# Inverse square roots as one GpSimd power operation, and the low halves of ten weight blocks made in the feed-forward before the mixers

## The chip, the cores and the metric

One core of a Trainium2 chip runs the whole program in one launch. The metric is the device time of one execution in microseconds (us); less is better. The kernel before takes 1023.36 us (median of 3 runs, 1023.26 to 1024.52).

## What is computed

Two layers act on x of 256 tokens by 1024 columns, in float32. Each layer is a feed-forward with half weight, three token mixers side by side, and a second feed-forward:

```
x = x + 0.5 * swiglu(rms_norm(x, norm_ffn1), ffn1_w13, ffn1_w2)     # 1024 -> 2 x 2816 -> 1024
h = rms_norm(x, norm_mix)
z, xbc, dt_raw, cq, ckv, kidx, widx, xl, gl = split(h @ w_in)       # 1024 -> 2508 columns
y = concat(ssd(z, xbc, dt_raw), attention(cq, ckv, kidx, widx), rg_lru(xl, gl))
x = x + y @ w_out
x = x + 0.5 * swiglu(rms_norm(x, norm_ffn2), ffn2_w13, ffn2_w2)
```

`rms_norm` multiplies by `rsqrt(mean(x*x) + 1e-6)`. It is used for the three norms of the layer, for cq, ckv and kidx (one number per token each), for the heads of q and k (8 per token), and for the two groups of the state-space mixer's output. The attention selects 64 keys per query by an indexer's score. The state-space mixer (SSD) convolves xbc, takes silu of it, and combines it with decays that come from a cumulated sum of softplus(dt_raw); the recurrence (rg_lru) is a scan over time.

## The kernel before

A float32 product is made from three fast products. Each weight tile is split (`wsplit`, L255) into a high half `whi`, a rounded copy by ScalarE (L260), and a low half `wlo`, the rest, by VectorE (L261); `mm3` and `mmt` (L250, L264) then add high times high, high times low and low times high in PSUM. `whi` and `wlo` have four buffers each, the landing place `wraw` of a weight load four as well (1 MB each); the SP queue issues the loads in program order, each as soon as its buffer is free.

A feed-forward (`ffn`, L316) goes over 11 pieces c of 256 columns, with two loads of 1 MB per piece, and then over the second weight in 12 loads. The mixers (`mixers`, L384) project the small columns first (dt, cq, ckv, kidx, widx; L417 to L429), and then, by `pair` (L407), eight pairs of blocks of 128 columns: xl, four pairs of xbc (columns 512, 768, 0 and 256 of it), gl, and two of z. Each block takes 24 products of 256 columns. A pair's sums stand in one of three PSUM buffers named gu until VectorE has multiplied them by the row norms (`scaled`, L685; L727; L773).

Beside these blocks run the small chains of the mixers. For the attention: the squares of cq, ckv and kidx (L438), their inverse roots `sc` (L454), the indexer's queries and keys (L473, L485, L493 to L496), their transposes (L506), scores (L523, L530), eight rounds of taking the eight largest (`select`, L534: MAX and MATCH_REPLACE on VectorE), then the mask, softmax and the weighted values (L592 to L625). For the SSD: a softplus on GpSimd in some thirty small steps (L634 to L639), the cumulated sum `pac` on TensorE (L641), the decays M0 and M1 (L647 to L666), the convolutions (L669), of which those of columns 512 and 768 are issued after the selection (`picked`), and the products with the decays. At the end come the out-projections (`project`, L804, matmuls on L807) and the next feed-forward.

An inverse root (`rsqrt`, L158, and `rsqrt_of`, L164) is a first guess from the bits of the number and two steps of Newton's kind, eleven instructions on VectorE counting the first scaling; for the heads of q and k it is on GpSimd, where two of the steps need an extra instruction each time.

The order on each engine is set when the program is built: a scheduler goes through the program text and a model of the engines' times and places each instruction; on the chip each engine then keeps that order strictly and waits where an operand is not there.

Of the kernel before, what the change touches and what calls it, by code (L numbers as in the profile page):

```python
# [7 lines left out]
F32 = mybir.dt.float32  # L8
# [7 lines left out]
P = 128  # L16
# [15 lines left out]
MAGIC = 1597463007.0  # L32
RS = (64.0 / 9.0) ** 2
# [31 lines left out]
def tile_decoder_trunk(ctx: ExitStack, tc: tile.TileContext, A: dict, out: bass.AP):  # L65
# [79 lines left out]


# [11 lines left out]
    def rsqrt(dst, src, scale, pool, tg, E=V):  # L158
# [5 lines left out]
    def rsqrt_of(dst, v, pool, tg, E=V):  # L164


        n = list(dst.shape)
        yi = pool.tile(n, I32, name=tg + "y")
        E.tensor_scalar(yi, v.bitcast(I32), -0.5, MAGIC, ALU.mult, ALU.add)
        v2 = pool.tile(n, F32, name=tg + "h")  # L170
        E.tensor_scalar(v2, v, 9.0 / 64.0, None, ALU.mult)
        y = yi.bitcast(F32)
        for i in range(2):
            t = pool.tile(n, F32, name=tg + "t")
            E.tensor_mul(t, y, y)
            E.tensor_mul(t, t, v if i == 0 else v2)
            stt(E, t, t, -10.0 / 3.0, t, ALU.add, ALU.mult)
            z = dst if i == 1 else pool.tile(n, F32, name=tg + "z")
            last = stt(E, z, t, 5.0, y, ALU.add, ALU.mult)
            y = z  # L180
        return last.ins
# [134 lines left out]
    def ffn(n, w13, w2, pool, finish, first=False):  # L316
# [5 lines left out]
        for c in range(KF // 2):  # L322
# [61 lines left out]
    def mixers(n, l, mp, finish):  # L384
# [5 lines left out]
        ya_, yl_ = two("ya_", 1), two("yl_", 1)  # L390

# [3 lines left out]
        def mix_ps():  # L395
            return psa.tile([P, 512], F32, name="acc")
# [10 lines left out]
        def pair(raw, c0, eng):  # L407
# [43 lines left out]
        for i, dim in enumerate((256, 128, 64)):  # L451
            V.tensor_scalar(vc[:, i], lss[:, i], RS / dim, EPS * RS, ALU.mult, ALU.add)
        sc = mp.tile([P, 3, NH], F32, name="sc", bufs=1)
        rsqrt_of(sc, vc, mp, "cr")  # L454
# [106 lines left out]
        rsqrt(qr, qss, 1.0 / 64, mp, "qq", G)  # L561
# [85 lines left out]
        M0, M1 = [], []  # L647
        for g in range(2):
            m0 = mp.tile([P, 4, SEQ], F32, name="m0", bufs=2)
            m1 = mp.tile([P, 4, P], F32, name="m1", bufs=2)  # L650
            for q in range(2):
                pb = mix_ps()
                for i in range(2):
                    hd = 4 * g + 2 * q + i
                    for h in range(NH):
                        bcast_rows(pb[:, i * SEQ + h * P:i * SEQ + (h + 1) * P], ac[:, h, hd:hd + 1])
                for i in range(2):
                    hd = 4 * g + 2 * q + i
                    S.activation(m0[:, 2 * q + i], pb[:, i * SEQ:(i + 1) * SEQ], AF.Relu, scale=-1.0,
                                 bias=ac[:, 0, hd:hd + 1])  # L660
                    S.activation(m1[:, 2 * q + i], pb[:, i * SEQ + P:(i + 1) * SEQ], AF.Relu, scale=-1.0,
                                 bias=ac[:, 1, hd:hd + 1])
            S.activation(m0, m0, AF.Exp, scale=-1.0)
            S.activation(m1, m1, AF.Exp, scale=-1.0)
            M0.append(m0)
            M1.append(m1)  # L666

# [22 lines left out]
        def xbc_pair(raw, b0, eng, after=None):  # L690
            xr = scaled(pair(raw, 0, eng))
            t = two("xbc", 4)
# [6 lines left out]
        def lru():  # L699
            ps = pair(load_cols(C_XL, 256), 0, (V, V))  # L700
            xr = two("lx", 1)
            conv(xr, scaled(ps), "lru_conv_w", 2, "lru_conv_b", 0)
            la, la2, lt, lb = two("la", 1), two("la2", 1), two("lt", 1), two("lb", 1)
# [20 lines left out]
        def lru_gate(hs):  # L724
            ps = pair(load_cols(C_GL, 256), 0, (V, V))
            gx, hx, gt = two("lx", 1), two("lb", 1), two("lt", 1)
# [8 lines left out]

        hs = lru()


        xbc_pair(load_cols(C_XBC + 512, 256), 4, (V, V), picked)
        xbc_pair(load_cols(C_XBC + 768, 256), 6, (V, V), picked)  # L740

        for g in range(2):
# [4 lines left out]
            cb = mp.tile([P, 3 * P], F32, name="cb", bufs=2)  # L747
# [4 lines left out]
        xbc_pair(load_cols(C_XBC, 256), 0, (V, V))  # L752
        xbc_pair(load_cols(C_XBC + 256, 256), 2, (V, V))

        xdt = []
        for h in range(NH):
# [3 lines left out]
            t = mp.tile([P, 8, 64], F32, name="xdt", bufs=2)  # L760
# [8 lines left out]
        zs, yg = [], []  # L769
        for q in range(2):  # L770
            ps = pair(load_cols(C_Z + 256 * q, 256), 0, (V, V))
            z = two("z", 2)
            V.tensor_mul(z, ps, rb2)  # L773
            silu2(z, z)
            zs.append(z)
# [163 lines left out]
```

## Time and profile before

| | |
|---|---|
| median of 3 runs | 1023.36 us |
| the profiled execution | 1025.87 us |
| its span in the trace | 1024.1 us |
| TensorE (PE) busy | 991.1 us, 97% |
| VectorE (DVE) busy | 661.3 us, 65% |
| ScalarE (ACT) busy | 515.2 us, 50% |
| GpSimd (POOL) busy | 52.7 us, 5% |

The profiled execution took 1025.87 us, of which 1024.1 us are its span, from the first instruction to the last, and 1.8 us lie around it. Matmuls are pipelined: their lengths overlap, so that the distance from one start to the next is what one costs. All times inside are counted from the start of the span. Layer 0's mixers lie at about 206 to 330 us, layer 1's at about 711 to 834 us.

### The profile page before, as it was taken

The numbers are of one execution on the slowest core, as the hardware profiler recorded it, in microseconds if no ns is written. First come the engines' busy times: TensorE is split into PE (matmuls) and PEld (weight loads), VectorE is DVE, ScalarE is ACT, GpSimd is POOL, SyncE is SP. The second block draws the span as 40 slices with busy tenths as digits, with TensorE's granted clock in tenths as the row PEclk, the third lists the DMA queues.
The fourth block names the chain that finished last, engine by engine and source line by source line (L and its number), as shares of the span: only waits on it lengthen the run. The fifth ranks groups of instructions, "written<-read, shape, count | busy, mean of one in ns | idle before, by whom it ended". The sixth has DMA issues, their size and how long they took to land.

```text
span 1024.1 us, 12885 instructions
## 1 busy us (share of the span) xinstructions
PE 991.1 (97%) x4819; PEld 806.0 (79%) x4819; DVE 661.3 (65%) x1158; ACT 515.2 (50%) x806; POOL 52.7 (5%) x133
## 2 busy tenths in 40 slices
PE   7999999999869999999999999999998999999998
PEld 5888888889844888888888888888897468888886
DVE  6666755576977666664576656555889766566543
ACT  6554545468533554544455445455695255454442
POOL 0600000042000000000000000000500000000000
PEclk9999999999989999999999999999998899999999
DMA  9765555743205565555556555557431256564560
GB/s 318 204 201 175 175 186 167 242 148 109 98 27 184 167 197 177 173 195 194 186 159 207 190 175 176 183 197 229 131 125 42 60 187 206 168 201 149 183 224 21
DMA packets 142752, 172.47 MB, mean 168 GB/s; under 512 B 4851, under 2 KB 114577, under 8 KB 142689
## 3 DMA queue, kind: packets, MB, share of 16 engines
q1 hardware_dynamic: 141792, 171.03, 51.9%
q0 software_dynamic: 864, 0.60, 0.4%
q8 instruction: 38, 0.62, 0.2%
q14 instruction: 26, 0.21, 0.1%
q10 hardware_dynamic: 32, 0.01, 0.0%
HBM read 170.57 MB, written 1.05 MB: 168 GB/s over the span
## 4 chain that ended last, share of the span: by engine, by line
PE 83%; DVE 9%; ACT 3%; DMA 2%; POOL 2%; issue 1%; SPq 0%; ACTq 0%; DVEq 0%; POOLq 0%
PE gu L266 16%; PE gu L268 16%; PE gu L267 16%; PE acc L267 8%; PE acc L268 8%; PE acc L266 8%; PE gu L807 3%; DVE wlo L261 2%; DMA wraw<-in_ffn_w_dram 2%; PE sm L356 2%; DVE xbc L674 1%; PE gu L251 1%; DVE score L542 1%; PE gu L253 1%; PE gu L252 1%; PE sm L289 1%
## 5 line engine op out<-in xcount | busy, mean ns | idle before, releaser
L261 DVE TENSOR_TENSOR wlo<-wraw,whi 128x1024 fp32r<-128x1024 f32 (+1 forms) x304 | 370.5, 1221 | 259.0 <-ACT whi L260 252.7
L260 ACT ACTIVATE whi<-wraw 128x1024 fp32r<-128x1024 f32 (+1 forms) x304 | 321.9, 1061 | 283.5 <-PE gu L268 159.3
L266 PE MATMUL gu<-whi,xh 128*128 128x512 f32 (+1 forms) x736 | 289.8, 396 | 2.5 <-ACT whi L260 2.5
L268 PE MATMUL gu<-whi,xl 128*128 128x512 f32 (+1 forms) x736 | 289.0, 396 | 0.0
L267 PE MATMUL gu<-wlo,xh 128*128 128x512 f32 (+1 forms) x736 | 286.6, 391 | 0.0
L267 PEld LDWEIGHTS gu<-wlo,xh 128*128 128x128 f32 x736 | 138.7, 189 | 28.2 <-DVE wlo L261 0.8
L266 PEld LDWEIGHTS gu<-whi,xh 128*128 128x128 f32 x736 | 138.6, 189 | 28.2 <-ACT whi L260 2.9
L268 PEld LDWEIGHTS gu<-whi,xl 128*128 128x128 f32 x736 | 138.5, 188 | 27.6
L268 PE MATMUL acc<-whi,hl 128*128 128x512 f32 x352 | 137.8, 392 | 0.0
L267 PE MATMUL acc<-wlo,hh 128*128 128x512 f32 x352 | 137.2, 390 | 0.0
L266 PE MATMUL acc<-whi,hh 128*128 128x512 f32 x352 | 135.7, 391 | 0.0
L251 PE MATMUL gu<-xh,whi 128*128 128x256 f32 x256 | 76.3, 298 | 6.3 <-DVE z L773 4.0
L351 ACT ACTIVATE th_s<-gu,rhalf 128x256 f32<-128x256 f32 x88 | 41.8, 475 | 75.9 <-PE gu L268 75.7
L267 PEld LDWEIGHTS acc<-wlo,hh 128*128 128x128 f32 x352 | 66.1, 188 | 13.7
L268 PEld LDWEIGHTS acc<-whi,hl 128*128 128x128 f32 x352 | 66.1, 188 | 13.6
L266 PEld LDWEIGHTS acc<-whi,hh 128*128 128x128 f32 x352 | 66.1, 188 | 13.4
L252 PE MATMUL gu<-xl,whi 128*128 128x256 f32 x256 | 75.4, 295 | 0.0
L253 PE MATMUL gu<-xh,wlo 128*128 128x256 f32 x256 | 75.1, 293 | 0.0
L251 PEld LDWEIGHTS gu<-xh,whi 128*128 128x128 f32 x256 | 50.1, 196 | 8.3 <-issue 5.3
L352 DVE SCALAR_TENSOR_TENSOR th_s<-th_s,gu 128x256 f32<-128x256 f32 x88 | 36.8, 418 | 27.9 <-ACT th_s L351 27.7
L252 PEld LDWEIGHTS gu<-xl,whi 128*128 128x128 f32 x256 | 50.3, 196 | 1.8 <-issue 1.4
L253 PEld LDWEIGHTS gu<-xh,wlo 128*128 128x128 f32 x256 | 50.2, 196 | 1.0 <-issue 0.5
(307 smaller groups left out, 835.1 us busy)
## 6 DMA issues: line engine op xcount, KB each, us to landing
wraw<-in_ffn_w_dram SPq DMA_DIRECT2D x180, 512.0 KB, 4.7
wraw<-in_ffn_w_dram SPq DMA_DIRECT2D x40, 1024.0 KB, 5.0
wraw<-in_w_in_dram SPq DMA_DIRECT2D x16, 1024.0 KB, 5.1
wraw<-in_w_out_dram SPq DMA_DIRECT2D x8, 1024.0 KB, 5.0
wraw<-in_w_in_dram SPq DMA_DIRECT2D x4, 920.0 KB, 4.7
wraw<-in_ffn_w_dram SPq DMA_DIRECT2D x8, 256.0 KB, 5.7
xr<-in_x_dram SPq DMA_DIRECT2D x4, 256.0 KB, 3.9
out_dram<-xr SPq DMA_DIRECT2D x4, 256.0 KB, 2.6
```

Source lines behind the costliest of these rows:

```text
L251: T.matmul(o, lh, rh, start=first, stop=False)
L252: T.matmul(o, lh, rl, start=False, stop=False)
L253: T.matmul(o, ll, rh, start=False, stop=last)
L260: S.activation(hi[sl], raw, AF.Copy)
L261: eng.tensor_sub(lo[sl], raw, hi[sl].bitcast(F32))
L266: T.matmul(o, xh, wh, start=first, stop=False)
L267: T.matmul(o, xh, wl, start=False, stop=False)
L268: T.matmul(o, xl, wh, start=False, stop=last)
L351: S.activation(th, ps[h][:, 0:256], AF.Tanh, scale=rh_[:, h:h + 1])
L352: V.scalar_tensor_tensor(th, th, 1.0, ps[h][:, 0:256], ALU.add, ALU.mult)
L356: T.transpose(pt[:, j * SEQ + h * P:j * SEQ + (h + 1) * P], hf[:, j * P:(j + 1) * P], ident)
L807: T.matmul(acc, y[:, h * P:(h + 1) * P], w, start=t == 0, stop=t == len(ys) - 1)
```

## The change

**The roots.** `rsqrt` scales on GpSimd, and `rsqrt_of` is one GpSimd instruction, a power with the exponent -0.5 from a constant tile `mhalf`. VectorE has no step of a root any more. The scalings by RS, which belonged to the first guess, go.

**The low halves.** During the first feed-forward of each layer, before the pieces c = 3, 5, 7, 9 and 10, `early_lows` loads 256 columns of `w_in` (1 MB) and makes two low halves of them, with the high half in the same tile for the moment between. The ten tiles (the pairs of xl and of xbc) are kept in a new pool `early` with ten buffers e of 4 KB per partition. In the mixers these five pairs are loaded again, ScalarE makes the high halves, and the low halves are there; gl and z are split as before.

**The buffers.** The tiles e are used again in the mixers in the same order: for the recurrence's la, la2, lt, lb, for M0 and M1, the convolved xbc, cb, xdt and z. M0 and M1 are written after the recurrence in the program text, not before it.

```
-        E.tensor_scalar(v, src, scale * RS, EPS * RS, ALU.mult, ALU.add)
-        return rsqrt_of(dst, v, pool, tg, E)
...
-        yi = pool.tile(n, I32, name=tg + "y")
-        E.tensor_scalar(yi, v.bitcast(I32), -0.5, MAGIC, ALU.mult, ALU.add)
-        v2 = pool.tile(n, F32, name=tg + "h")
-        E.tensor_scalar(v2, v, 9.0 / 64.0, None, ALU.mult)
-        y = yi.bitcast(F32)
-        for i in range(2):
-            t = pool.tile(n, F32, name=tg + "t")
-            E.tensor_mul(t, y, y)
-            E.tensor_mul(t, t, v if i == 0 else v2)
-            stt(E, t, t, -10.0 / 3.0, t, ALU.add, ALU.mult)
-            z = dst if i == 1 else pool.tile(n, F32, name=tg + "z")
-            last = stt(E, z, t, 5.0, y, ALU.add, ALU.mult)
-            y = z
+        G.tensor_scalar(v, src, scale, EPS, ALU.mult, ALU.add)
+        return rsqrt_of(dst, v)
+
+    def rsqrt_of(dst, v):
...
+        return G.tensor_tensor(dst, v, e, op=ALU.pow).ins
...
+    EARLY = [C_XL] + [C_XBC + c for c in (512, 768, 0, 256)]
+
+    def early_lows(l, ep, i):
+        raw = rp.tile([P, KD, 256], F32, name="wraw")
+        nc.sync.dma_start(raw, A["w_in"][l][:, EARLY[i]:EARLY[i] + 256].rearrange("(k p) c -> p k c", p=P))
+        lows = []
+        for j in range(2):
+            e = ep.tile([P, KD, P], F32R, name="e")
+            r = raw[:, :, j * P:(j + 1) * P]
+            S.activation(e, r, AF.Copy)
+            V.tensor_sub(e, r, e.bitcast(F32))
+            lows.append(e)
+        return lows
...
+            if aside and c in (3, 5, 7, 9, 10):
+                aside(min(c // 2 - 1, 3) if c < 10 else 4)
...
-                w = wsplit([P, KD, P], [(slice(None), raw[:, :, c0 + j * P:c0 + (j + 1) * P])], eng[j])
+                r = raw[:, :, j * P:(j + 1) * P]
+                if c0 in EARLY:
+                    hi = wp.tile([P, KD, P], F32R, name="whi")
+                    S.activation(hi, r, AF.Copy)
+                    w = hi, lows[EARLY.index(c0)][j]
+                else:
+                    w = wsplit([P, KD, P], [(slice(None), r)], V)
                 block(ps[:, j, :], w)
...
-        rsqrt_of(sc, vc, mp, "cr")
+        rsqrt_of(sc, vc)
...
+        with tc.tile_pool(name=f"early_{l}", bufs=10, reuse_waits="tile") as ep:
```

**What moves.** The order is made anew, and two places of it matter below. The first is VectorE in the eight rounds of the selection, layer 0 (score and m are the score tables and the eight largest of them, wlo the low halves, lt, lb and la the recurrence's tiles). Before, a low half stands in nearly every round:

```order
L539 MAX m_2036<-score_2032 128x8
L539 MAX m_2013<-score_2010 128x8
L542 MATCH_REPLACE score_2040<-m_2036,score_2032 128x256
L542 MATCH_REPLACE score_2018<-m_2013,score_2010 128x128
L717 SCALAR_TENSOR_TENSOR lt<-la_2379,lt 128x512
L539 MAX m_2044<-score_2040 128x8
L539 MAX m_2021<-score_2018 128x8
L261 TENSOR_TENSOR wlo<-wraw,whi 128x1024
L542 MATCH_REPLACE score_2048<-m_2044,score_2040 128x256
L542 MATCH_REPLACE score_2026<-m_2021,score_2018 128x128
L719 SCALAR_TENSOR_TENSOR lb<-lt,lb 128x512
```

Now the rounds follow each other with nothing between:

```order
L560 MAX m_2055<-score_2051 128x8
L560 MAX m_2032<-score_2029 128x8
L563 MATCH_REPLACE score_2059<-m_2055,score_2051 128x256
L563 MATCH_REPLACE score_2037<-m_2032,score_2029 128x128
L560 MAX m_2063<-score_2059 128x8
L560 MAX m_2040<-score_2037 128x8
L563 MATCH_REPLACE score_2067<-m_2063,score_2059 128x256
L563 MATCH_REPLACE score_2045<-m_2040,score_2037 128x128
L569 SCALAR_TENSOR_TENSOR ya<-score_2067,inv_200 128x256
```

and the six low halves that are left in the mixers, those of gl and z, come after the selection, among the mask and softmax (mx, sums), the convolutions (cx into e) and gl's read from PSUM (lx<-gu), all of which stand ahead of them or behind them in this one queue:

```order
L252 TENSOR_TENSOR wlo<-wraw,whi 128x1024
L674 SCALAR_TENSOR_TENSOR e<-cx,colT_107,e 128x254 x4
L614 TENSOR_REDUCE mx<-rel 128x4
L622 RECIPROCAL sums<-sums 128x4
L252 TENSOR_TENSOR wlo<-wraw,whi 128x1024
L674 SCALAR_TENSOR_TENSOR e<-cx,colT_107,e 128x253 x2
L252 TENSOR_TENSOR wlo<-wraw,whi 128x1024
L674 SCALAR_TENSOR_TENSOR e<-cx,colT_107,e 128x253 x2
L730 TENSOR_TENSOR lx<-gu,nrb 128x512
L616 SCALAR_TENSOR_TENSOR mx<-mx,qr 128x4
L252 TENSOR_TENSOR wlo<-wraw,whi 128x1024
L640 TENSOR_TENSOR ya<-sm,sums 128x256
```

The second place is GpSimd in the softplus of layer 0 (sp tiles; the last row shown is its first polynomial step). Before:

```order
L154 TENSOR_TENSOR spa<-stt_2213,dtx 128x16
L191 TENSOR_SCALAR spd<-spe 128x16
L202 TENSOR_SCALAR spa<-dtx 128x16
L194 TENSOR_TENSOR sps<-spe,spd 128x16
L196 TENSOR_TENSOR spq<-sps 128x16
L198 TENSOR_SCALAR spc<-spq 128x16
```

Now the scalings of the squares (vc) and the power (sc<-vc,mhalf) stand in the same queue, ahead of the softplus's product sps:

```order
L155 TENSOR_TENSOR spa<-stt_2194,dtx 128x16
L473 TENSOR_SCALAR vc<-lss 128x2
L182 TENSOR_SCALAR spd<-spe 128x16
L193 TENSOR_SCALAR spa<-dtx 128x16
L473 TENSOR_SCALAR vc<-lss 128x2 x2
L172 TENSOR_TENSOR sc<-vc,mhalf 128x6
L185 TENSOR_TENSOR sps<-spe,spd 128x16
L187 TENSOR_TENSOR spq<-sps 128x16
L189 TENSOR_SCALAR spc<-spq 128x16
```

On TensorE the three-product matmuls that stand between the first use of cs and the indexer's first scores (L523 before, L544 now) are 44 fewer than before, the 14 transposes of the cumulated sum that stood there come later, and one pair of the recurrence's gates (L707) comes earlier; the attention's scores and everything behind them thus stand nearer to the front. The order of the blocks (xl, xbc, gl, z) is the same.

## Rows read from the trace of the kernel before

**Rows 1.** The profile page, part 4: shares of the chain that ended last.
```profile
PE 83%; DVE 9%; ACT 3%; DMA 2%; POOL 2%; issue 1%; SPq 0%; ACTq 0%; DVEq 0%; POOLq 0%
```

**Rows 2.** Busy time by stretch: window, length, PE, PEld, DVE, ACT, POOL, PEclk, DMA, GB/s.
```profile
82.00:137.00 55.00, 55.00 (x252) 45.00 (x251) 36.33 (x67) 25.84 (x35) 0.00 (x0) 1.00 0.55 176
214.00:245.00 31.00, 29.85 (x208) 26.40 (x207) 21.79 (x52) 20.53 (x45) 17.93 (x47) 0.94 0.39 121
245.00:296.00 51.00, 39.59 (x295) 36.33 (x294) 49.92 (x128) 33.18 (x70) 0.00 (x0) 0.94 0.22 72
...
230.00:236.00 6.00, 4.98 (x29) 4.99 (x30) 3.86 (x10) 1.80 (x3) 3.46 (x9) 0.72 0.56 176
```

**Rows 3.** TensorE's timeline, layer 0: start, length, line, output and input [idle before, releaser].
```profile
213.99 0.38 PE L445 MATMUL sm<-ident,cs 128*128 128x128 f32 x2
...
217.87 0.28 PE L251 MATMUL gu<-xh,whi 128*128 128x256 f32 x1
...
217.99 0.28 PE L252 MATMUL gu<-xl,whi 128*128 128x256 f32 x1
...
231.02 0.39 PE L641 MATMUL acc<-adt,tri 128*128 128x8 f32 x2 [1.15 <-POOL adt L638]
...
242.00 1.57 PE L523 MATMUL sm<-ck,qiT 64*128 64x256 f32 x12
...
273.44 0.35 PE L251 MATMUL gu<-xh,whi 128*128 128x256 f32 x1 [1.99 <-DVE z L773]
...
293.20 0.69 PE L623 MATMUL sm<-ident,ya 128*128 128x128 f32 x2 [5.07 <-DVE ya L619]
...
294.35 3.16 PE L807 MATMUL gu<-wraw,ya__1794 128*128 128x512 f32 x4 [0.46 <-ACT ya__1794 L625]
...
299.06 1.04 PE L759 MATMUL acc<-ident,xbc 128*128 128x128 f32 x8
...
322.21 4.13 PE L807 MATMUL gu<-wraw,lb 128*128 128x512 f32 x9 [0.88 <-DVE xr L812]
```

**Rows 4.** TensorE's timeline, layer 1.
```profile
735.56 0.39 PE L641 MATMUL acc<-adt,tri 128*128 128x8 f32 x2 [0.28 <-POOL adt L638]
...
745.06 1.57 PE L523 MATMUL sm<-ck,qiT 64*128 64x256 f32 x12
...
796.55 3.78 PE L807 MATMUL gu<-wraw,ya__6119 128*128 128x512 f32 x4 [0.46 <-ACT ya__6119 L625]
...
802.74 1.04 PE L759 MATMUL acc<-ident,xbc 128*128 128x128 f32 x8
```

**Rows 5.** VectorE by line: low halves in 206 to 246, then three groups of 245 to 296.
```profile
L261 DVE TENSOR_TENSOR wlo<-wraw,whi x11: 1157/1225/1226, 204.8 to 245.3; 128x1024 fp32r<-128x1024 f32 x11
...
L261 DVE TENSOR_TENSOR wlo<-wraw,whi 128x1024 fp32r<-128x1024 f32 x6 | 7.3, 1225 | 3.4 <-ACT whi L260 3.4
L542 DVE MATCH_REPLACE8 score<-m,score 128x256 f32<-128x256 f32 (+1 forms) x16 | 5.6, 355 | 0.0
...
L539 DVE MAX8 m<-score 128x8 f32<-128x256 f32 (+1 forms) x16 | 5.4, 361 | 0.1
```

**Rows 6.** VectorE's and GpSimd's timelines, layer 0.
```profile
219.39 1.16 DVE L261 TENSOR_TENSOR wlo<-wraw,whi 128x1024 fp32r<-128x1024 f32 x1
...
219.55 1.07 POOL L194 TENSOR_TENSOR sps<-spe,spd 128x16 f32<-128x16 f32 x1 [1.75 <-DVE spd L192]
220.70 0.21 POOL L196 TENSOR_TENSOR spq<-sps 128x16 f32<-128x16 f32 x1
...
234.20 0.20 POOL L169 TENSOR_SCALAR qqy<-qqv 128x16 int32<-128x16 int32 x1
...
239.46 0.22 POOL L156 TENSOR_TENSOR qr<-stt,qqz 128x16 f32<-128x16 f32 x1
```

**Rows 7.** DMA issues of the page, and waits of 60 to 200 us.
```profile
wraw<-in_w_in_dram SPq DMA_DIRECT2D x16, 1024.0 KB, 5.1
...
ACT whi L260 <- PE gu L268: 26.7, 21, 2.9
```

More of the change, by code (lines that the diff above doesn't have):

```diff
@@ L144, in tile_decoder_trunk @@
     hb = cp.tile([P, 2, 4], F32, name="hb")
+    mhalf = cp.tile([P, 32], F32, name="mhalf")
+    G.memset(mhalf, -0.5)
     def stt(E, out, a, sc, b, op0, op1):
@@ L381, in ffn, with mixers @@
                         finish(h, c)
-    def mixers(n, l, mp, finish):
+    def mixers(n, l, mp, ep, lows, finish):
         w_in = A["w_in"][l]
@@ L390, in mixers, with halves @@
         ya_, yl_ = two("ya_", 1), two("yl_", 1)
+        def halves(parts=2):
+            t = ep.tile([P, 1024], F32, name="e")
+            n_ = 1024 // parts
+            return [t[:, i * n_:(i + 1) * n_].rearrange("p (a b) -> p a b", a=2) for i in range(parts)]
         def att_ps():
@@ L688, in scaled, with xbc_pair @@
             return xr
-        def xbc_pair(raw, b0, eng, after=None):
-            xr = scaled(pair(raw, 0, eng))
-            t = two("xbc", 4)
+        xbcs = []
+        def xbc_pair(b0, after=None):
+            xr = scaled(pair(C_XBC + b0 * P))
+            if not xbcs:
+                xbcs.extend(halves())
+            t = xbcs.pop(0)
             with tc.issue_after(after) if after else nullcontext():
@@ L699, in lru @@
         def lru():
-            ps = pair(load_cols(C_XL, 256), 0, (V, V))
-            xr = two("lx", 1)
+            ps = pair(C_XL)
+            xr = lx
             conv(xr, scaled(ps), "lru_conv_w", 2, "lru_conv_b", 0)
-            la, la2, lt, lb = two("la", 1), two("la2", 1), two("lt", 1), two("lb", 1)
             for b in range(2):
@@ L724, in lru_gate @@
         def lru_gate(hs):
-            ps = pair(load_cols(C_GL, 256), 0, (V, V))
-            gx, hx, gt = two("lx", 1), two("lb", 1), two("lt", 1)
+            ps = pair(C_GL)
+            gx, hx, gt = lx, lb, lt
             V.tensor_mul(gx, ps, rb2)
@@ L750, in mixers @@
             V.tensor_mul(M1[g], M1[g], cb[:, None, SEQ:].to_broadcast([P, 4, P]))
-        xbc_pair(load_cols(C_XBC, 256), 0, (V, V))
-        xbc_pair(load_cols(C_XBC + 256, 256), 2, (V, V))
+        xbc_pair(0)
+        xbc_pair(2)
         xdt = []
+        xdts = ep.tile([P, NH, 8, 64], F32, name="e")
         for h in range(NH):
@@ L766, in mixers @@
         lru_gate(hs)
-        zs, yg = [], []
+        zs, yg = halves(), []
         for q in range(2):
[L771 to L775, printed above, removed]
+            ps = pair(C_Z + 256 * q)
+            V.tensor_mul(zs[q], ps, rb2)
+            silu2(zs[q], zs[q])
         for q in range(2):
-            y = two(("la", "la2")[q], 1)
+            y = (la, la2)[q]
             for j in range(2):
@@ L788, in mixers @@
             V.tensor_mul(y, y, zs[q])
-            yn = two(("lt", "lb")[q], 1)
+            yn = (lt, lb)[q]
             for j in range(2):
@@ L824, in mixers @@
         for q in range(2):
-            sq = two("z", 2)
+            sq = zs[q]
             S.activation(sq, yg[q][0], AF.Square)
```

103 lines of the change are left out of this document (56 added, 47 removed).

## The prediction

> **What bounds the kernel now.** I read the chain of waits first: TensorE holds 83% of it, VectorE 9% [rows 1]. So TensorE's work sets the time, except in stretches where VectorE holds it up. The table by stretch says where these lie [rows 2]: in a feed-forward (82 to 137 us) TensorE is busy for 55.00 of 55 us with VectorE at 36.33; in the mixers of layer 0, from 245 to 296 us, TensorE has 39.59 of 51 and VectorE 49.92. There VectorE is the bound. TensorE's timeline then gives the single waits [rows 3]: 1.15 us for GpSimd's softplus at 231, 1.99 at 273 for a PSUM buffer that VectorE had not read, 5.07 at 293 and 0.46 at 294 for the attention's output; with three smaller ones that the same timeline shows they make some 12.6 us between the transposes at 213.99 and the first out-projection at 294.35. After the wait at 231 the granted clock of 230 to 236 us is 0.72: TensorE ran for part of it at the lower level (1.2 instead of 2.4 GHz), and 0.28 x 6 = 1.7 us were lost [rows 2]. From 294 on TensorE is busy almost throughout.
>
> **What the change takes from VectorE, and why it is not simply 11 us.** A low half costs 1.22 us, of which 1.13 lie start to start. Of the mixers' sixteen, the ten that go away stand before 245 us, where VectorE has gaps (21.79 busy of 31); the six of the saturated stretch stay [rows 2, 5]. So the gain is not the ten times 1.13 us. It has to come from two things: what stood behind the ten starts earlier, and the six no longer cut up the selection.
>
> **Step 1, up to the scores.** TensorE now has 44 three-product matmuls and 14 transposes less ahead of the first scores, and one gate pair more. Start to start a matmul is 0.12 us [rows 3], so 44 x 0.12 = 5.3; the transposes are 0.112 each by the same timeline, 1.6; the pair costs 0.75. That is 6.1 us earlier. The wait for the softplus should go as well. Its GpSimd step sps lasted 1.07 us and began while a low half ran on VectorE; the step after it, which met none, lasted 0.21 [rows 6]. Without low halves there, the five steps of 1 us or more in this chain shrink to about 0.25 each, some 4 us; what is put into it, two scalings (0.3 each) and a power, fills a gap of 1.75 us that the row of sps shows. So adt should be there before TensorE asks for it, and the 1.15 us and the 1.7 us of clock go: 2.8 us. The scores then start at 242.0 - 6.1 - 2.8 = 233.1 in layer 0; in layer 1 the wait was only 0.28 [rows 4], so 745.1 - 6.1 - 0.3 = 738.7.
>
> **Step 2, VectorE from the scores to gl.** VectorE gets the first score 2.2 us after TensorE starts on them. From there to the reading of gl's sums (lx<-gu) I add what the new order puts in between, at start-to-start prices: 16 MAX and 16 MATCH_REPLACE with their loads, 9.8 us (12.5 busy, overlaps taken off) [rows 5]; scores 2.7; the recurrence 2.8; masks, maxima and marks 4.1; five of the six low halves 5.7; twelve convolution steps 4.7; two PSUM reads 1.2. Sum 31.0, and 1.1 for waits on ScalarE, which is nearly full here: 32.1. So gl's buffer is free 34.3 us after the scores start. TensorE would be there some 2.5 us before, and z's four blocks need that buffer: this wait is the one that is late next, in the place of the 1.99 us before.
>
> **Step 3, z and the rest.** 96 matmuls of z at 0.12 are 11.5 us; the attention's transposes and values and the SSD's products between them add 3.7. The first out-projection starts 34.3 + 15.2 = 49.5 us after the scores: at 282.6 in layer 0 (294.35 before, 11.7 less) and at 788.2 in layer 1 (796.55 before, 8.4 less). The attention's last values, VectorE's other late output, I get 4 us before TensorE asks for them.
>
> **Step 4, the clock behind it.** The first out-projection group took 4.7 us in layer 0 and 6.2 in layer 1 [rows 3, 4], the next of the same size 3.5: TensorE came out of waits at the lower level. Without the 5 us wait, 1.2 and 2.7 us go.
>
> **Step 5, the root at the mixers' end.** Ten VectorE steps become one power between two engines. The out-projections behind it wait 0.88 us at 322 for VectorE [rows 3], which at that moment is at a low half that waited for a load; the load is issued as before. I count nothing; if the power took over 3 us, this cover would be gone. The roots of the layer norms feed a tanh six us later and count nothing either.
>
> **Step 6, the feed-forward.** Each layer gets five more loads of 5.1 us, 10 copies on ScalarE and 10 low halves on VectorE; on the SP queue each load passes ahead of later weight loads. I cost them at nothing: TensorE has no idle time there, VectorE 18.7 us in 55, and ScalarE's high halves wait for TensorE to free a buffer (26.7 us of waits, the longest 2.9, in 60 to 200) [rows 2, 7]. ScalarE and VectorE are thus three to four tiles of 2.7 us ahead, and one early pair sets them back by 2.3. If the cover were gone, the price would be up to 2.3 x 10 = 23 us.
>
> **The power itself.** No row shows one. Below, it costs what any step on so small a tile does, 0.21 us; above, I take the whole chain that it replaces on GpSimd, 234.20 to 239.68, 5.5 us [rows 6]. I take 1 us, nearer to the single steps because it is a single instruction on the same 2 to 16 elements. Up to about 3.5 us it stays hidden at its three places per layer (behind the softplus, ahead of the first score, ahead of the last projections), so the sum takes it at nothing; at 5.5 it costs 3 x 5.5 - 10.5 = 6 us per layer. The Trainium skill (GPSIMD Engine Reference, Engine selection) says the opposite of this edit: small arithmetic belongs on VectorE, since GpSimd is about twice as slow on two inputs. By that rule alone the ten removed steps would each cost double; the rows show one step at 0.21 us there, and one instead of eleven.
>
> **The sum.** 11.7 + 8.4 + 1.2 + 2.7 = 24.0 us. From it I take what steps 2 and 3 leave out. The new wait for gl's buffer can bring the lower clock: of the waits of 1 to 2 us some did and some did not (231 did, 273 did not), so half of 1.7 us per layer. And queues that keep their order lose time in waits that I can't see from before; I take 1.5 us per layer. 24.0 - 2 x 2.35 = 19.3. Of the profiled execution's 1025.87 us 1006.6 are left; the median of the runs lies 2.5 below that execution, so 1004 us.
>
> **The rivals.**
> - *ScalarE takes over.* It has 33 us of work in 245 to 296 [rows 2], and now the decays M0 and M1, the recurrence and the attention's copies all fall between scores and mask. If it delays the mask by some 5 us per layer, the gain is 19 - 10: 1013 us. For it: two table loads of 1.3 us stand in its way. Against it: it was full from 242 to 260 before, too.
> - *The order buys little.* The six low halves of the saturated stretch stay. If the scores' earlier start is lost again, only the softplus's wait, its clock and step 4 are left: 2.8 + 0.3 + 1.2 + 2.7, less the friction of 4.7: 1021 us. Against it: TensorE's list of work ahead of the scores is shorter by count.
> - *The power is long: slower than before.* GpSimd would hold sc, then the heads' roots, which stand ahead of the first score on VectorE, then the last projections. At p us per power it costs 3p - 10.5 per layer; from p = 7 on the 19.3 us are eaten up, and at 10 us the time is 1004 + 2 x 19.5 = 1043. For it: nothing in the trace bounds a power. Against it: it would have to be longer than the chain that it replaces. A power that holds memory would also stop VectorE. The Trainium skill (SBUF — State Buffer, Who interferes with whom) says that a GpSimd instruction and a VectorE instruction with two inputs in SBUF lock each other out, the first one winning; the trace agrees for VectorE's side (1.07 against 0.21 us), and by it a long power would cost VectorE its own length too.
> - *The early loads are not hidden.* With c = 9 and 10 next to each other the loads come 1.5 times as densely; 10 to 23 us would come back: 1014 to 1027 us.
>
> **How the numbers follow.** Forecast 1004 us, chance 0.62. ScalarE takes over 0.20, the order buys little 0.06, the power is long 0.07, the loads show 0.05. If all waits of both mixers and all lost clock went, 29 us, the time would be 994; I set the low end at 996. The high end takes in the ScalarE rival: 1014. About 2 us (0.2%) is what a measurement of this kernel can tell from no change. Faster: the first three cases and part of the last, 0.90; same 0.03; slower 0.07.
>
> **What would show it.** Right: the first scores near 233 and 739 us; no low half inside the selection; the first out-projection near 283 to 286 and 789 to 792; TensorE without idle time from 30 to 200 us; GpSimd's steps all near 0.25 us, the power near 1. Wrong: a power above 3.5 us, waits of TensorE for adt or for the logits' copies, idle TensorE near 130 us, or a first out-projection later than 290.

## The result and the profile after

| | before | after |
|---|---|---|
| median | 1023.94 us (4 runs, 1023.26 to 1026.76) | 1008.60 us (4 runs, 1008.41 to 1009.64) |
| ratio | | 0.9847 [0.9827, 0.9867] |
| the profiled execution, its span | 1025.87 us, 1024.1 | 1008.49 us, 1006.8 |

The median before is of four runs here; the 1023.36 us that the forecast starts from were three of them. The change saves 15.3 us by the medians and 17.3 us of span between the two traces, since the profiled execution before lies 1.9 us above its median and the one after lies at it; 1004 us were forecast, in a range of 996 to 1014. The page's part 4, shares of the chain, after (it answers to [rows 1]):

```profile
PE 87%; DVE 5%; ACT 4%; DMA 3%; issue 1%; SPq 0%; ACTq 0%; DVEq 0%
```

VectorE's share falls from 9% to 5%, and GpSimd, which takes over the roots, leaves the chain. Busy time by stretch, with the columns of [rows 2]:

```profile
82.00:137.00 55.00, 55.00 (x253) 45.06 (x252) 40.62 (x72) 29.75 (x38) 0.00 (x0) 1.00 0.69 222
60.00:200.00 140.00, 140.00 (x637) 115.22 (x637) 89.44 (x127) 72.31 (x93) 0.00 (x0) 1.00 0.65 212
214.00:245.00 31.00, 31.00 (x222) 27.06 (x221) 20.44 (x59) 23.28 (x52) 13.75 (x38) 1.00 0.33 103
...
268.00:274.00 6.00, 5.19 (x24) 5.19 (x25) 6.00 (x15) 3.23 (x11) 0.00 (x0) 0.50 0.76 280
```

The feed-forward hides its extra work: TensorE is busy for 140.00 of 140 us at full clock. From 214 to 245 it has no gap left, where before 1.15 us and some clock were lost. The stretch 268 to 274 is new: clock 0.50, the lower of the two levels. TensorE's timeline after, layer 0 and from 729 us layer 1 (answering to [rows 3, 4]), shows what stands ahead of it:

```profile
214.08 0.38 PE L466 MATMUL sm<-ident,cs 128*128 128x128 f32 x2
...
228.60 0.49 PE L527 MATMUL sm<-ident,sqc 128*128 128x128 f32 x3
...
233.63 1.57 PE L544 MATMUL sm<-ck,qiT 64*128 64x256 f32 x12
...
268.81 0.58 PE L242 MATMUL gu<-xh,whi 128*128 128x256 f32 x1 [2.91 <-DVE lx L730]
269.19 0.41 PE L243 MATMUL gu<-xl,whi 128*128 128x256 f32 x1
269.40 0.41 PE L244 MATMUL gu<-xh,wlo 128*128 128x256 f32 x1
...
285.93 1.45 PE L835 MATMUL gu<-wraw,ya__1811 128*128 128x512 f32 x3
...
729.22 1.14 PE L544 MATMUL sm<-ck,qiT 64*128 64x256 f32 x8
...
764.40 0.58 PE L242 MATMUL gu<-xh,whi 128*128 128x256 f32 x1 [2.91 <-DVE lx L730]
...
781.22 1.88 PE L835 MATMUL gu<-wraw,ya__6051 128*128 128x512 f32 x4
```

I cut each mixer at four marks of TensorE (the anchor is the first transpose of cs, at 213.99 and 719.40 us before, 214.08 and 709.67 after; the last is the norm sums of the SSD, matmuls with `ones`), and write the lengths before and after:

| stretch | layer 0 | layer 1 | gain |
|---|---|---|---|
| anchor to first scores | 28.01, 19.55 | 25.66, 19.55 | 14.6 |
| scores to first out-projection | 52.35, 52.30 | 51.49, 52.00 | -0.5 |
| out-projection to `ones` | 19.06, 17.95 | 20.54, 17.96 | 3.7 |

The three gains add up to 17.8 us; everything else in the program gives back 0.5. So nearly all of it stands ahead of the scores, and between the scores and the out-projection, where the selection now has no low halves in it, nothing is gained. The products that no longer stand ahead of the scores are not gone: they come later, where TensorE used to wait. From the anchor to `ones`, both layers together, TensorE sits idle for 20.5 us before and 7.4 after, and has the lower clock for 23.9 us before and 13.7 after; the idle time and half of the time at the lower clock make 18.2 us (an estimate, from these sums), close to the 17.8.

### The profile page after: what moved, and what is told of

Read it like the earlier page. It is cut to its first block, busy times and chain, and to the rows that moved or that the text cites. A ratio compares the mean times of both kernels' runs of the same rounds, so it can differ in the third digit from the quotient of the medians.

```text
span 1006.8 us, 12816 instructions
## 1 busy us (share of the span) xinstructions
PE 986.4 (98%) x4819; PEld 805.0 (80%) x4819; DVE 648.6 (64%) x1046; ACT 533.0 (53%) x826; POOL 52.7 (5%) x130
## 3 DMA queue, kind: packets, MB, share of 16 engines
HBM read 181.06 MB, written 1.05 MB: 181 GB/s over the span
## 4 chain that ended last, share of the span: by engine, by line
PE 87%; DVE 5%; ACT 4%; DMA 3%; issue 1%; SPq 0%; ACTq 0%; DVEq 0%
PE gu L258 16%; PE gu L257 16%; PE gu L259 16%; PE acc L257 8%; PE acc L258 8%; PE acc L259 8%; PE gu L835 3%; DVE wlo L252 2%; DMA wraw<-in_ffn_w_dram 2%; PE gu L242 2%; PE gu L243 2%; PE sm L364 2%; PE gu L244 2%; PE sm L280 1%; DVE e L674 1%
## 5 line engine op out<-in xcount | busy, mean ns | idle before, releaser
L252 DVE TENSOR_TENSOR wlo<-wraw,whi 128x1024 fp32r<-128x1024 f32 (+1 forms) x284 | 345.6, 1220 | 222.4 <-ACT whi L251 214.9
L251 ACT ACTIVATE whi<-wraw 128x1024 fp32r<-128x1024 f32 (+1 forms) x284 | 299.1, 1059 | 249.7 <-PE gu L259 135.3
L244 PE MATMUL gu<-xh,e 128*128 128x256 f32 x160 | 46.0, 288 | 0.0
L362 DVE TENSOR_TENSOR hf<-th_s,gu 128x256 f32<-128x256 f32 x88 | 36.9, 421 | 2.9
```

The lines of the kernel that those rows point to most:

```text
L244: T.matmul(o, ll, rh, start=False, stop=last)
L251: S.activation(hi[sl], raw, AF.Copy)
L252: eng.tensor_sub(lo[sl], raw, hi[sl].bitcast(F32))
L362: V.tensor_mul(hf, th, ps[h][:, 256:512])
```

## The experiments

Each ran beside the kernel before on the same chip; the ratios in the text are to that, with their 95% intervals.

### Which half of the change does it?

Two kernels take the change apart. The first keeps the early low halves and has the old roots, on VectorE (those of the heads on GpSimd):

```
-        return G.tensor_tensor(dst, v, e, op=ALU.pow).ins
+        yi = pool.tile(n, I32, name=tg + "y")
+        E.tensor_scalar(yi, v.bitcast(I32), -0.5, MAGIC, ALU.mult, ALU.add)
...
+            last = stt(E, z, t, 5.0, y, ALU.add, ALU.mult)
```

> The changed kernel with the eleven-step inverse square roots of before (VectorE; GpSimd for the heads) in place of the powers: the early low halves and the new order alone. Theory A (the low halves carry the gain, the powers buy little, because the root chains lie beside other work): 1009 to 1012 us, so at least four fifths of the 15.3 us between 1023.9 and 1008.6 stay. Rival B (the powers carry a good part, since VectorE loses ten steps in front of the scores, of the last projections and of each feed-forward): 1014 to 1018 us. Then the trace should show TensorE waiting in front of the scores (240 in the place of 233.6 us) or 2 us and more in front of the last projections.

It took 1016.17 us, 0.9918 [0.9904, 0.9932]. The second is the kernel before with every root as a power, and no early low half:

> The kernel before with the powers alone; all sixteen low halves are made in the mixers. Theory A: 1021 to 1025 us, no gain that can be measured: the mixers' waits of TensorE (1.15 us for adt, 5.07 and 2.92 us for the attention's output) stay. It may lose a little: the power of six elements (1.36 us) goes into GpSimd's chain ahead of adt, for which TensorE already waits 1.15 us, so that wait should grow to 2 to 3 us. Rival B (the powers carry part of the gain): 1014 to 1019 us.

It took 1009.70 us (1005.47 to 1011.16), 0.9845 [0.9826, 0.9863]: the whole gain. Against the 1025.18 of the kernel before on that chip the roots alone give 15.5 us and the low halves alone 9.0; both together gave 15.3. The halves do not add; with the roots in, the early low halves are worth nothing that these runs show. VectorE's timeline of the kernel before tells where they meet, in the stretch between vc, the scaled squares of cq, ckv and kidx, and their root sc (eleven steps on tiles cry, crh, crt, crz):

```profile
220.47 0.24 DVE L452 TENSOR_SCALAR vc<-lss 128x2 f32<-128x2 f32 x2
220.84 1.23 DVE L261 TENSOR_TENSOR wlo<-wraw,whi 128x1024 fp32r<-128x1024 f32 x1
221.99 0.17 DVE L169 TENSOR_SCALAR cry<-vc 128x6 int32<-128x6 int32 x1
...
224.14 0.15 DVE L176 TENSOR_TENSOR crt<-crt,vc 128x6 f32<-128x6 f32 x1
224.22 0.86 DVE L674 SCALAR_TENSOR_TENSOR lx<-cx,colT,lx 128x253 f32<-128x253 f32 x2
...
227.02 0.69 DVE L687 TENSOR_TENSOR cx<-gu,nrb 128x512 f32<-128x512 f32 x1 [0.53 <-PE gu L253]
227.63 0.15 DVE L150 SCALAR_TENSOR_TENSOR sc<-crt,crz 128x6 f32<-128x6 f32 x1
...
233.10 0.35 DVE L496 TENSOR_TENSOR sqc<-rp,rp 128x192 f32<-128x192 f32 x1
```

Each step lasts 0.15 to 0.18 us, yet the root takes from 221.99 to 227.78, since convolutions (lx), products and a PSUM read stand between the steps in VectorE's one queue. The indexer's vectors sqc (the last row shown finishes them), their transposes and the scores hang on sc. After the change, GpSimd's and VectorE's timelines:

```profile
217.77 1.36 POOL L172 TENSOR_TENSOR sc<-vc,mhalf 128x6 f32<-128x6 f32 x1
219.10 0.22 POOL L185 TENSOR_TENSOR sps<-spe,spd 128x16 f32<-128x16 f32 x1
...
219.16 0.62 DVE L506 SCALAR_TENSOR_TENSOR sqc<-cs,sc,kig 128x128 f32<-128x128 f32 x2 [0.33 <-POOL sc L172]
```

sc is there 8.7 us earlier. But on the chip TensorE waited for none of this, not even before. Its timeline before:

```profile
237.62 0.38 PE L506 MATMUL sm<-ident,sqc 128*128 128x128 f32 x2
```

The transposes run 4.2 us after the last part of sqc is done (233.45), with no wait in front of them; between anchor and scores TensorE waits only for the softplus, 1.15 us in layer 0 and 0.28 in layer 1. What holds the scores back is the list: 137 block products stand between anchor and scores before, 96 after (41 fewer, not the 44 of the text above), 114 with the roots alone and 94 with the low halves alone. The scheduler makes this list from its model of the times, so that the chain of sc counts where the model sees it; how it weighed it is not on record. Either half frees VectorE's queue ahead of sc (ready 13.8 us behind the anchor before, 5.1 after, 6.1 with the roots alone, 9.2 with the low halves alone), and either moves the scores: to 19.55 us behind the anchor after the change, 20.84 with the roots alone, 20.18 with the low halves alone. That is one gain, reached by two ways.

The three differ in what comes behind the scores. With the low halves alone the out-projection starts 55.40 us after the scores in layer 0 and 51.83 in layer 1: TensorE waits 2.06 us for the copies prob in both, then 3.25 and 0.50 us for ya, with the lower clock for longer in layer 0. The heads' root is still a chain on GpSimd there; what part of this is due to it the run does not show. With the roots alone it is 48.85 us in both layers, less than the 52.30 and 52.00 after the change, although low halves still stand between the rounds of the selection. By the three stretches of the table the roots alone gain 12.0, 6.1 and 0.4 us: as much as the change, but not in the same places.

### Is it one root, and is it the data or the list?

Here only sc is a power in the kernel before; in its complement all others are, and sc keeps its eleven steps:

```
-            V.tensor_scalar(vc[:, i], lss[:, i], RS / dim, EPS * RS, ALU.mult, ALU.add)
+            G.tensor_scalar(vc[:, i], lss[:, i], 1.0 / dim, EPS, ALU.mult, ALU.add)
...
-        rsqrt_of(sc, vc, mp, "cr")
+        G.tensor_tensor(sc, vc, mhalf.rearrange("p (a b) -> p a b", a=3), op=ALU.pow)
```

> The kernel before with one root by a power: sc, the three per-token roots of cq, ckv and kidx. All other roots and all low halves as before. Theory E (new, after the powers alone gave the whole gain): sc gates the scores. In the kernel before its eleven steps stand in VectorE's queue between low halves and convolution steps, from the last vc at 220.47 to sc at 227.78 us; behind it come kidx, its rotation and the transposes (237.62); with the powers sc is there at 220.1 and the transposes come at 229.67, the scores at 234.56 in the place of 242.0. So this one root should give most: scores near 235, 1009 to 1014 us. Rival F (the heads' root, 5.5 us of GpSimd before and 2.94 as a power, or the last root's steps on VectorE carry the gain): 1018 us or more.

> The complement: the kernel before with all roots by powers but sc, which keeps its eleven steps on VectorE. Theory E: scores near 242 as before, 1019 to 1025 us. Rival F: 1010 to 1015 us.

sc alone took 1016.45 us, 0.9908 [0.9891, 0.9926]; its complement 1023.50, 0.9982 [0.9971, 0.9992]. The scores come at 20.84 us with sc alone, as with all roots, and at 25.59 without it. The first edit touches sc and its scaling and nothing else, and shortens TensorE's list ahead of the scores from 137 to 114 block products; the second leaves it at 137. But 8.7 and 1.7 us do not make 15.5. With sc alone, VectorE's wait for the heads' root qr, then TensorE's timeline at its wait for the attention's transposed weights pT, and the stretch behind that:

```profile
238.09 0.69 DVE L568 TENSOR_TENSOR qk<-qk,qr 128x512 f32<-128x512 f32 x1 [1.71 <-POOL qr L565]
```

```profile
264.97 3.33 PE L619 MATMUL sm<-vt,pT 128*128 128x64 f32 x15 [3.44 <-ACT pT L614]
```

```profile
266.00:270.00 4.00, 4.00 (x20) 4.00 (x20) 4.00 (x8) 2.81 (x5) 0.00 (x0) 0.50 0.06 6
270.00:274.00 4.00, 4.00 (x26) 4.00 (x26) 4.00 (x10) 2.48 (x9) 0.00 (x0) 0.68 0.74 260
```

and the last two views with all roots as powers, where VectorE does not wait for qr:

```profile
263.66 0.44 PE L609 MATMUL sm<-vt,pT 128*128 128x64 f32 x2 [1.63 <-ACT pT L604]
```

```profile
266.00:270.00 4.00, 4.00 (x35) 4.00 (x35) 4.00 (x9) 1.42 (x3) 0.00 (x0) 1.00 0.32 84
270.00:274.00 4.00, 4.00 (x36) 4.00 (x35) 4.00 (x11) 3.52 (x12) 0.00 (x0) 1.00 0.47 182
```

With the heads' root still in its long chain, VectorE waits 1.71 us for it, the mask comes 1.8 us later counted from the scores, the wait for pT is 3.44 instead of 1.63 us, and from 266 to 274 us TensorE runs 46 matmuls instead of 71. The late root costs its delay and the clock; it shows only once the scores are early.

The next kernel has no power at all. In the kernel before, it holds a convolution, the heads' products and one pair's low halves back until sc is done, so that the eleven steps run in one piece:

```
+        rooted = rsqrt_of(sc, vc, mp, "cr")
...
+            with tc.issue_after(rooted): V.tensor_mul(qk[:, h, 0:4], pq4, qg[:, l, None, :].to_broadcast([P, 4, 64]))
...
+            with tc.issue_after(rooted): conv(xr, xs_, "lru_conv_w", 2, "lru_conv_b", 0)
```

> The kernel before with no power and all low halves as they were: only VectorE's order is changed, so that the eleven steps of sc stand in one run. The convolution of lx, the first products for q and the low halves of the third pair wait for sc. Theory E (what the power took away is the place of these steps between work of 0.4 to 1.2 us each, not the steps' own length): sc near 222 in the place of 227.78, scores near 236 in the place of 242.0, 1012 to 1018 us, about as with sc alone as a power (1016.5). Rival (the steps themselves, or the low halves that now come later for TensorE, cost as much): 1021 us or more.

It took 1027.43 us, 1.0027 [1.0016, 1.0038]: slower, and my expectation was wrong. VectorE's and TensorE's timelines of this kernel:

```profile
220.88 0.17 DVE L150 SCALAR_TENSOR_TENSOR sc<-crt,crz 128x6 f32<-128x6 f32 x1
```

```profile
235.97 0.38 PE L506 MATMUL sm<-ident,sqc 128*128 128x128 f32 x2
...
241.40 1.57 PE L523 MATMUL sm<-ck,qiT 64*128 64x256 f32 x12
```

sc came 6.7 us earlier (221.05 against 227.78), the scores only 0.6. In TensorE's list of this kernel 144 block products stand ahead of the scores, seven more than before, and an engine does not pass its own list. So this does not test the early sc with the list as it was; moreover the last part of sqc was done only 2.4 us earlier (231.09 against 233.45), behind low halves in VectorE's queue, and lay ready 4.9 us before its transposes. What it shows is that an early operand alone gave nothing here, since the consumer's list did not move forward with it. In the change the list did move; that it did so because the scheduler's model knew the short root is likely, but not shown.

### What does a power cost, and is it hidden?

Groups of the power's line after the change, by tile: count; shortest, median and longest duration in ns; first and last start in us; shape:

```profile
L172 POOL TENSOR_TENSOR nr<-nqv,mhalf x6: 695/697/730, 8.5 to 818.3; 128x2 f32<-128x2 f32 x6
L172 POOL TENSOR_TENSOR sc<-vc,mhalf x2: 1352/1356/1359, 217.8 to 713.4; 128x6 f32<-128x6 f32 x2
L172 POOL TENSOR_TENSOR qr<-qqv,mhalf x2: 2936/2936/2936, 231.2 to 726.8; 128x16 f32<-128x16 f32 x2
L172 POOL TENSOR_TENSOR yr<-yv,mhalf x2: 1028/1028/1029, 305.1 to 800.4; 128x4 f32<-128x4 f32 x2
```

The longest, for the heads, holds VectorE up: after the change it waits 2.20 us for qr, at 234.49 in layer 0. The first score behind that is not there yet either (VectorE then waits another 0.24 us for it), so this wait is covered. To test the cover, the power is issued twice everywhere:

```
-        return G.tensor_tensor(dst, v, e, op=ALU.pow).ins
+        G.tensor_tensor(dst, v, e, op=ALU.pow); return G.tensor_tensor(dst, v, e, op=ALU.pow).ins
```

> The changed kernel with every power computed twice, one behind the other, same values. In the trace of the changed kernel a power takes 0.70 us on 2 elements, 1.03 on 4, 1.36 on 6 and 2.94 on 16, so this adds up to 6.0 us of GpSimd time per layer and norm. Theory A (hidden up to about 3.5 us at each place): the heads' power becomes 5.9 us and passes that bound by 2.4, VectorE's wait for it (2.20 us) grows to some 5, and the last projections (wait 0.95) come 1 us later: 1 to 3.5 us per layer, 1010 to 1016 us. Rival (no power is near any path): 1008 to 1010 us. Rival (they are already on the path): 6 us per layer, 1020 us.

It took 1012.31 us, 0.9874 [0.9861, 0.9887], so 3.7 us more than after, for 5.3 us of extra power per layer at sc, heads and last root (1.36 + 2.94 + 1.03). The order on the engines changed with it (scores 19.67 us behind the anchor, pT waited for by 0.98 us), so this is the price of a schedule with twice the power, not of the power alone.

### Can the late wait be had back?

After the change TensorE waits 2.91 us for gl's sums to be read (lx<-gu, L730), and VectorE has low halves of z in front of that read. The first kernel moves z's low halves behind it, which takes three out of the way; the second (`read[0] if q else None`) only those of z's second pair, one low half:

```
+            read.append(V.tensor_mul(gx, ps, rb2).ins)
...
-            ps = pair(C_Z + 256 * q)
+            ps = pair(C_Z + 256 * q, read[0])
```

> The changed kernel; the low halves of the four blocks of z are put behind VectorE's reading of gl's sums (lx<-gu), three of them move. In the changed kernel TensorE waits 2.91 us for that reading in each layer, and then runs its next 26 matmuls at the lower clock (granted 0.50), 0.21 instead of 0.12 us each, 2.4 us more. Theory C (this wait and the clock behind it are what the forecast was short of): wait below 1 us, no lower clock behind it, 3 to 5 us less per layer: 999 to 1003 us. Rival D (VectorE is the bound there, so what is moved behind the reading comes late for z, or the attention's output does): the wait moves to a low half of z or to the attention's output, 1006 to 1010 us.

> The changed kernel; one single low half (the first of z's second pair) is moved from before to behind VectorE's reading of gl's sums, 1.13 us. The run that moved three of them gained at this wait and lost as much at the next, for the attention's output, which lay over 2 us and had the lower clock behind it. Theory J (the waits' length beyond some 2 us is what costs, by the clock: 1.63 and 1.99 us were followed by the full clock, 2.91 and 3.44 by half): the wait shrinks to 1.8 us, the 26 matmuls behind it run at 0.12 us, and a wait for the attention's output appears, below 2 us: 2 to 3.5 us less per layer, 1001 to 1005 us. Rival D (VectorE's order only moves the waits): 1007 to 1012 us.

They took 1011.95, 0.9872 [0.9859, 0.9885], and 1008.28, 0.9834 [0.9819, 0.9849]: 3.3 us slower than after, and no different from it. In the first the wait for lx shrank to a wait of 0.41 us for a low half, but the attention's output, behind the same low halves in VectorE's queue, came late. TensorE's timeline of the first:

```profile
283.55 0.44 PE L644 MATMUL sm<-ident,ya 128*128 128x128 f32 x2 [2.82 <-DVE ya L640]
```

In the second the wait for lx was 1.78 us and the matmuls behind it still ran at the lower clock, so the theory of the expectation failed; the 1.15 us of the kernel before, with the lower clock behind it, was against it already. From anchor to `ones` its mixers are 1.3 us shorter per layer than after the change, but the time is not: the wait for xr behind the last root was 1.92 us in layer 0 (0.95 after the change) and 1.59 in layer 1 (1.48), and where the rest went is not shown. Another kernel makes other blocks' low halves early, gl's and z's first pair instead of two pairs of xbc:

```
-    EARLY = [C_XL] + [C_XBC + c for c in (512, 768, 0, 256)]
+    EARLY = [C_XL, C_XBC + 512, C_XBC + 256, C_GL, C_Z]
```

> The changed kernel with another choice of the ten early low halves: xl, two pairs of xbc (512, 256), gl and the first pair of z, in the place of xl and the four pairs of xbc. Two low halves in the place of six are then left between the scores and the last value of the attention on VectorE; those of the xbc pairs 768 and 0 are made ahead of the scores. Theory G (with the powers in, VectorE's work from the scores to the attention's output sets the end of the mixers; low halves that stood ahead of the scores were worth nothing there, those behind them are worth their 1.13 us each): 4 x 1.13 x 2 = 9 us less at most, 1000 to 1004 us. Rival H (another chain ends last there, or what is now ahead of the scores makes these later): 1006 to 1012 us.

It took 1014.94, 0.9899 [0.9884, 0.9914], slower than every theory of mine had it: the low halves returned ahead of the scores, which started 21.92 us behind the anchor, and lx and ya were still waited for (2.80 and 2.58 us). The change run again, as a yardstick on that chip:

> The changed kernel once more, on the same chip as the three others, so that they can be set against it: 1007 to 1010 us by every theory.

1008.99 us, 0.9833 [0.9817, 0.9850]. Against this run the other's mixers are 2.3 us longer, both layers together, and its span 4.5 us; what lies outside the mixers is not explained.

### A version that beats both

With the roots alone TensorE waits 2.20 us for ya. On VectorE the products of the decays M0 and M1 with cb stand ahead of ya, though the SSD needs them later. They are issued behind the last ya (M1 in the same way), once with the roots alone and once with z's low halves behind lx:

```
-            V.tensor_mul(M0[g], M0[g], cb[:, None, :SEQ].to_broadcast([P, 4, SEQ]))
+            with tc.issue_after(weighed): V.tensor_mul(M0[g], M0[g], cb[:, None, :SEQ].to_broadcast([P, 4, SEQ]))
...
```

> The kernel before with the powers alone (1009.7 us), and one more move: VectorE's last product of the attention (ya<-sm,sums) goes ahead of the two mask products of the SSD that stood before it (1.21 and 0.68 us); TensorE's and ScalarE's lists are the same row for row. In the run with the powers alone TensorE waited 2.20 us for that ya and 0.46 for its copy, and ran the first out-projections at a granted clock of 0.50 and 0.69 (284 to 288 us). Theory G (VectorE's order from the scores on sets the end of the mixers, and the clock multiplies its waits): the wait shrinks to below 0.6 us, the clock stays at 1.00, 2.5 to 3.5 us less per layer: 1002 to 1006 us. Rival (what is moved behind makes the SSD's products late instead, or the clock does not depend on this wait): 1008 us or more.

> The changed kernel with three low halves of z behind the reading of gl's sums (1011.95 us), and the same further move of ya ahead of the SSD's mask products. There the wait for gl's sums was gone (2.91 to 0.41 us with the clock at 1.00), but TensorE then waited 2.82 us for ya and had a clock of 0.50 and 0.65 behind it. Theory G: that wait shrinks below 1 us and the clock stays: 3 to 4 us less per layer, 1003 to 1006 us, below the changed kernel's 1008.6 to 1009.0. Rival: 1009 us or more.

The first took **1005.63 us** (5 runs, 1004.30 to 1006.57), 0.9804 [0.9788, 0.9820]. All its runs lie below all eight of the change, which ran on other chips (1006.86 to 1009.64). Its interval lies below that of the roots alone, though the runs of the two overlap, and between their two traces the span differs by 1.1 us only: the mixers are 2.2 us shorter in layer 0, and 0.6 longer in layer 1, where the clock fell (last section). The second took 1008.96, 0.9839 [0.9824, 0.9854], 3.0 us less than without the move, and short of what I expected of it. TensorE's timeline of the first, in layer 0 and layer 1:

```profile
264.03 2.26 PE L609 MATMUL sm<-vt,pT 128*128 128x64 f32 x16 [1.63 <-ACT pT L604]
...
281.16 0.44 PE L616 MATMUL sm<-ident,ya 128*128 128x128 f32 x2 [0.49 <-DVE ya L612]
...
286.70 1.17 PE L752 MATMUL acc<-ident,xbc 128*128 128x128 f32 x8 [0.95 <-DVE xbc L674]
...
757.59 0.43 PE L609 MATMUL sm<-vt,pT 128*128 128x64 f32 x2 [1.63 <-ACT pT L604]
```

The wait for ya falls from 2.20 to 0.49 us and the clock stays at 1.00 from 280 to 290 (0.73 in 282 to 286 with the roots alone); the wait of 0.95 for xbc is new: VectorE finishes it no earlier than with the roots alone, and TensorE is there sooner.

## Why the prediction was right, and where it was wrong

**Step 1, the size: right.** The scores were forecast 8.9 us earlier in layer 0 and 6.4 in layer 1, counted from the start of the mixers; 8.46 and 6.11 were measured. The wait for the softplus is gone, and GpSimd's steps of it from 219 to 227 us last 0.21 to 0.39 us. Of the five steps that the forecast calls 1 us or more, two were shorter in the trace before (0.98 and 0.81); their sum still exceeds five of 0.25 by 4.2 us.

**Step 1, the cause: half wrong.** The step that failed is the paragraph ahead of it, which says that the gain "has to come from two things: what stood behind the ten starts earlier, and the six no longer cut up the selection", with the roots counted at nothing. The first of the two is real, since the low halves alone bring the scores to 20.18 us and save 9.0 us; but the roots alone save 15.5, as much as both together (15.3). I read the 44 matmuls off the new order without asking which edit had moved them. The chain of sc was in the trace of before: steps of 0.15 us, stretched over 5.8 us, ahead of the scores. I summed the steps that go and did not look at what stands behind their result in the order. The second of the two things gave nothing: -0.5 us between scores and out-projection.

**Step 2: right in size.** gl's buffer was forecast free 34.3 us after the scores, with a wait of 2.5; it was 35.2 (233.63 to 268.81) and 2.91. Only the total was measured, not the terms of that sum.

**Steps 3 and 4.** From there to the out-projection 15.2 us were forecast; it took 17.1 (268.81 to 285.93). The clock is enough to explain the difference: in layer 0 some 26 matmuls behind the wait ran at 0.213 us start to start instead of 0.12, about 2.4 us, where I had taken half of 1.7. The 3.9 us behind the out-projection came (3.7).

**Step 5.** Right at the place it names. The last root, ten steps from 314.40 to 316.33 before, is one power of 1.03 us on GpSimd (305.1 us), and VectorE still waits for TensorE behind it (its timeline after):

```profile
304.87 0.16 DVE L860 TENSOR_SCALAR yv<-sm 128x4 f32<-128x4 f32 x1
306.76 0.75 DVE L840 SCALAR_TENSOR_TENSOR xr<-gu,yr,xr 128x512 f32<-128x512 f32 x1 [1.73 <-PE gu L835]
```

**Step 6: right.** No idle time of TensorE from 60 to 200 us; the early loads are hidden, and, as the run with the roots alone shows, bought nothing once the roots are powers.

**The power.** 1 us was taken; it is 0.70 to 2.94, by the number of elements per partition, inside the bounds of 0.21 and 5.5 and below the 3.5 at which the forecast lets the cover end; no run measured that bound by itself. Behind the four medians lies about 0.38 us and 0.16 per element (an estimate, from these rows). The Trainium skill (GPSIMD Engine Reference, Engine selection) puts elementwise add, multiply and max on VectorE, with GpSimd about twice as slow on two inputs. It compares single instructions. No run here has the same two-input one on both engines; the scaling vc, with one input, took 0.16 us on VectorE before and 0.19 on GpSimd after. What counted here was eleven places in a full queue against one instruction on an engine that is busy for 5% of the span.

**The sum.** 24.0 less 4.7 of friction were forecast, 17.3 of span measured. The 4.8 us that step 3 had between scores and out-projection and the friction of 4.7 cancel on paper and did so on the chip (-0.5); the 2.0 us left over are the scores (0.7), the out-projections (0.2), that stretch (0.6), and 0.5 outside the mixers. So two uncertain terms offset each other, and that part of the agreement is luck. The forecast time is 4.6 us off rather than 2.0, because it takes another 2.5 from the profiled execution to the median, as before; after the change the two agree (1008.49 and 1008.60). And the cause that the forecast names, taken alone, gives the 1016.17 us of the low halves alone, above its range: the time came near by the roots, which it counts at nothing.

**The rivals.** ScalarE did not take over: after the change TensorE waits for it 0.48 us per layer, for the copies prob, and another 0.2 for pT. That the order buys little, that the power is long and that the loads show all failed.

## What to carry to other kernels

When a chain of tiny steps goes, measure it from its input to its result, in the queue in which it stands, not by the sum of its steps, and look for who hangs on the result and where that stands in its engine's list. Where two edits clear the same queue ahead of the same consumer, their gains can overlap: try each alone before keeping both, since here the cheaper one, which needs no second load of ten blocks, is as fast. An operand that comes earlier pays only when the consumer's place in its own engine's list moves too.

## What was not expected of the hardware

**The same wait, once with and once without the clock.** In the best kernel TensorE has the same list in both layers and waits 1.63 us for pT in both (rows above). Stretches of 4 us behind that wait in layer 0, and of 2 us in layer 1:

```profile
266.00:270.00 4.00, 4.00 (x35) 4.00 (x35) 4.00 (x9) 1.79 (x3) 0.00 (x0) 1.00 0.24 45
...
760.00:762.00 2.00, 2.00 (x11) 2.00 (x11) 2.00 (x5) 0.44 (x2) 0.00 (x0) 0.50 0.00 0
762.00:764.00 2.00, 2.00 (x11) 2.00 (x11) 2.00 (x6) 0.92 (x2) 0.00 (x0) 0.50 0.56 186
```

From this wait to the transposes of ya TensorE takes 17.13 us in layer 0 and 19.95 in layer 1. Over these kernels the length of a wait did not tell: 1.15 us (before, at 231) and 1.78 were followed by the lower level, 1.99 (before, at 273) and 2.80 were not. That this also makes the spread between runs of one kernel (1005.47 to 1011.16 with the roots alone, at mean clocks of 0.996 to 0.991) fits, but was not shown. What decides stays open.

**Low halves slow GpSimd's small steps.** This was forecast, and holds. With the roots alone one of the softplus's steps (221.00 to 222.05 us) met a low half on VectorE (220.71 to 221.94) and lasted 1.05 us, and its like without one 0.34; after the change, with no low half there, none of the softplus's steps is above 0.39. The Trainium skill (SBUF — State Buffer, Who interferes with whom) says that a VectorE instruction with two inputs in SBUF and a GpSimd instruction that reads SBUF contend, and that the one issued second waits for the first to end; the trace agrees, the step ending 0.11 us after the low half.
